# A third pair of places for split weight halves in two mixers, taken from tiles that lose their second buffer

## The chip, the core and the metric

The kernel runs on one core of a Trainium2 chip. Its time is the device time of one execution in microseconds (us); several executions are given by their median. TensorE (PE) multiplies matrices, VectorE (DVE) and ScalarE (ACT) work element by element, GpSimd (POOL) does little here, and SyncE (SP) issues the transfers from HBM.

## The reference, cut to what matters

The model runs 256 tokens of width 1024 through two blocks. The first block (a gated linear attention with pooling, then a mixture of 32 experts) takes the first 850 us and holds nothing of what this change is about. The second block has two layers. Each is a mixer and then a feed-forward part:

```python
p = x_normed @ w_in                    # 1024 -> 3788 columns, split into 16 parts
o_delta = gated_deltanet(q, k, v, z, b, a, ...)    # convolution of 4 taps and silu on q, k, v; then
    # chunks of 64: T = inverse(I + strict(beta k k^T decay)), u0 = T (beta v), wk = T (beta e^G k)
    # a scan over 4 chunks: u = u0 - wk S; o = q_dec S + (q k^T decay) u; S = g S + k_dec^T u
o_sparse = dsa_attention(q, k, v, qi, ki, wi)      # scores of an indexer, top 64, softmax
o_gated  = hgrn2(q, f, i, g, lb, norm_g)           # gated linear attention, chunks of 64
x = x + norm(concat(o_delta, o_sparse, o_gated) @ w_out)
x = x + norm(conv_geglu_ffn(norm(x)))
```

All of it is in float32 and has to be accurate to float32.

## The kernel before

A product in full precision on PE would take four passes, so `dense` and `down` split both operands into a high and a low half of a reduced type (fp32r) and add three products: high x high, high x low, low x high. The activations are split once per layer (`hh`, `hl`). The weights come through a ring of 1 MB tiles `w` of 128 x 2048, one for each group of 256 output columns, and each tile is split in two halves of 128 x 1024 that ACT and DVE make: `hl` hands out a pair (`whi`, `wlo`), `split` has ACT copy the weight to `whi` (line 175, which rounds) and DVE subtract it for `wlo` (line 177). One half feeds 24 matmuls of 256 columns (4 of the 8 groups of 128 input rows, two blocks of 128 outputs or tokens, three products), so a step of 256 columns has 48. The pair comes from the pool `spl`, which holds two of them: a new split waits for the matmuls that read the pair two splits earlier.

A mixer is written as a list of steps, among them the dense ones: k0, k1, q0, q1, v0, v1 (the delta rule's, with a convolution at their end), z0, z1, qi, bq, ci, cq, cg, and steps of work between: gates, inv (the inverse by doubling, matrices of 128 x 128), rest and chunks (the delta rule), sp0, sp1 (the sparse attention), hg (the gated linear attention). `order` gives each step a priority, and a scheduler then sorts the instructions of each engine by priority among those whose operands and buffers are ready. A change of the number of buffers thus changes the order on every engine. Each engine works off its queue in order, and an instruction that waits holds up everything behind it.

Four steps of a mixer matter below. At its start PE runs k0 and k1 while ACT computes the delta rule's gates (`E`, `eG` and others, lines 1596 to 1614). In `ci` the result of a dense step is copied from PSUM by ACT (line 1550). A convolution (`conv`, lines 1453 to 1460) takes a result out of PSUM in ACT and DVE, in part through a tile `raw`. In hg, six levels (2, 4, 8, 16, 32 and 64 tokens) each multiply `hq` by `hk` into two PSUM banks, and DVE copies the results under a mask into `hA` (lines 1906 and 1908), after it made the next level's `hq` and `hk` (lines 1912 to 1921).

The PSUM banks of a mixer are dealt out by user: `dense=(0, 1), delta=(2, 3, 4), hgrn=(5, 6), sparse=(7, 6), out=(0, 1, 6, 7)`. All other tiles of a mixer lie in the pool `mp`, with one buffer for each tag unless said.

Of the kernel before, what the change touches and what calls it, by code (L numbers as in the profile page):

```python
# [9 lines left out]
F32 = mybir.dt.float32  # L10
F32R = mybir.dt.float32r
BF16 = mybir.dt.bfloat16
# [5 lines left out]
P = 128  # L18
# [46 lines left out]
class K:  # L65
# [96 lines left out]
    normed0, first = None, []  # L162

    def diag(self, r, first=None):
        dg = self.sml.tile([P, P], F32, name="dg", tag="dg", bufs=2)
        ins = self.nc.vector.tensor_scalar(dg, self.c("ident"), r, None, op0=OP.mult).ins
        if first in self.hold:
            self.normed0 = ins
        return dg
# [3 lines left out]
    def split(self, hi, lo, src):  # L173

        self.nc.scalar.copy(hi, src)  # L175
        with self.tc.issue_after(self.normed0) if self.normed0 else contextlib.nullcontext():
            self.nc.vector.tensor_sub(lo, src, hi.bitcast(F32))  # L177

    def hl(self, shape):
        hi = self.spl.tile([P, 1024], F32R, name="whi", tag="whi")  # L180
        lo = self.spl.tile([P, 1024], F32R, name="wlo", tag="wlo")
        n = shape[0] * shape[1]
        return [t[:, :n].rearrange("p (j c) -> p j c", j=shape[0]) for t in (hi, lo)]

# [1180 lines left out]

    def ffn(self, l, fp, hh, hl, hu, rb):
        nc, v = self.nc, self.v2[l]
        self.ring(dense=(0, 1, 2, 3), out=(4, 5, 6, 7), pre=(2, 3))
        self.tmp = lambda name: fp.tile([P, D], F32, name=name, tag=name, bufs=2)
        late = lambda: fp.tile([P, 2048], F32, name="late", tag="late", bufs=self.lates[1] - 2)  # L1370
        self.late = lambda: (lambda t: (t[:, :D], t[:, D:]))(late())
        uv = self.i["ffn_w_up_2"][l].rearrange("(p j) c -> p j c", j=KJ)

        other = "AB"[self.side == "A"]
        self.wbig = lambda: self.big("w", other, F32).rearrange("p j t -> p (j t)")
        self.first = ["b"] * 2
        dh, dl = (fp.tile([P, 22, S], F32R, name=n) for n in ("dh", "dl"))
        for s in range(11):
            cv = fp.tile([P, 4, S], F32, name="cv", tag="cv", bufs=2)

            def ev(a, q):
                for b in range(2):
                    n = 22 * q + 2 * s + b
                    self.conv(cv[:, 2 * q + b, :], a[:, b, :], [v["fconv"][:, k, n:n + 1] for k in range(3)])
            for q in range(2):
                pc, e = [(q * D_FF + s * 256, 256)], lambda a, q=q: ev(a, q)
                if s < self.plain:
                    def scaled(a):
                        o = self.tmp("xg")[:, :512].rearrange("p (n t) -> p n t", n=2)
                        nc.vector.tensor_tensor(o, a, rb[:, None, :].to_broadcast([P, 2, S]), op=OP.mult)  # L1390
                        e(o)
                    self.dense32(self.wtile(), uv, pc, hu, scaled)
                else:
                    self.dense(uv, pc, (hh, hl), e)
            self.gelu = nc.scalar.activation(cv[:, :2, :], cv[:, :2, :], AF.Gelu_apprx_tanh).ins
            nc.vector.tensor_tensor(cv[:, 2:, :], cv[:, :2, :], cv[:, 2:, :], op=OP.mult)
            d0, d1 = dh[:, 2 * s:2 * s + 2, :], dl[:, 2 * s:2 * s + 2, :]
            nc.scalar.copy(d0, cv[:, 2:, :])
            nc.vector.tensor_tensor(d1, cv[:, 2:, :], d0.bitcast(F32), op=OP.subtract)
        dv = self.i["ffn_w_down_2"][l].rearrange("(j p) c -> p j c", p=P)  # L1400
        return self.down(dv, range(22), dh, dl, "g_ffn_post_2", l, "g_mix_pre_2", l + 1, self.lates[1])
# [60 lines left out]
    def mixer(self, l, mp, hh, hl, hu, rb):  # L1462
        nc, v = self.nc, self.v2[l]
        V = nc.vector
        self.mp = mp
        self.ring(**self.banks)
        self.now = (self.order, self.order2)[l]
        self.tmp = lambda name: T(name, (D,), tag="d4", bufs=N_D4)
# [50 lines left out]
        def load(n, u):  # L1519
            def ev(a):  # L1520
                for b in range(2):
                    c = 2 * u + b
                    self.conv(qkv[n][:, c, :], a[:, b, :],
                              [v["conv"][:, k, 4 * n + c:4 * n + c + 1] for k in range(4)],
                              T("raw", (S,), bufs=2) if b else None)
                x = qkv[n][:, 2 * u:2 * u + 2, :]
                self.silu2(T, x, x)
            self.dense(wv, [(512 * n + 256 * u, 256)], X, ev)
# [99 lines left out]
    def delta_inverse(self, T, kT, gt):  # L1628
# [34 lines left out]
        for m in (1, 2, 4, 8, 16, 32):  # L1663
            for t in range(2):
                ps = self.bk("delta")
                for h in range(4):
                    if m == 1:
                        nc.tensor.transpose(ps[:, h * P:(h + 1) * P], N[:, t, h, :], ident)
                    else:
                        nc.tensor.matmul(ps[:, h * P:(h + 1) * P], N[:, t, h, :], U[:, t, h, :], start=True, stop=True,  # L1670
                                         skip_group_check=True)
                if m == 1:
                    put(Ti[:, t], N[:, t], "lt1", m, 0)
                    put(U[:, t], hv(ps), "lv1", m, 1)
                    continue
                Z = T("Z", (4, P), tag="s2", bufs=4)
                nc.scalar.copy(Z, hv(ps))
                pt, pu = self.bk("delta") if m < 32 else None, self.bk("delta")
                for h in range(4):
                    if m < 32:  # L1680
                        nc.tensor.matmul(pt[:, h * P:(h + 1) * P], Z[:, h, :], Ti[:, t, h, :], start=True, stop=True,  # L1681
                                         skip_group_check=True)
                    nc.tensor.matmul(pu[:, h * P:(h + 1) * P], Ti[:, t, h, :], Z[:, h, :], start=True, stop=True,  # L1683
                                     skip_group_check=True)
                if m < 32:
                    put(Ti[:, t], hv(pt), f"lt{m}", m, 0)
                put(U[:, t], hv(pu), f"lv{m}", m, 1)
# [57 lines left out]
    def delta_chunks(self, T, v, dn, sz, oh, ol):  # L1745
# [6 lines left out]
        for n in range(4):  # L1752
            t, r = n // 2, slice(64 * (n % 2), 64 * (n % 2) + 64)
            u = u0[:, t]
            if St is not None:
                ps = self.bk("delta")
                for h in range(4):
                    nc.tensor.matmul(hv(ps)[r, h, :], wk[:, t, h, r], St[:, h, :], start=True, stop=True,  # L1758
                                     skip_group_check=True)
                V.tensor_tensor(u[r], u[r], hv(ps)[r], op=OP.subtract)  # L1760
            if n < 3:
                ps = self.bk("delta")
                for h in range(4):
                    nc.tensor.matmul(hv(ps)[:, h, :], kd[r, t, h, :], u[r, h, :], start=True, stop=True,
                                     skip_group_check=True)
                S2 = T("S", (4, P), tag="s2", bufs=4)
                if St is None:
                    nc.scalar.copy(S2, hv(ps))
                else:
                    for h in range(4):  # L1770
                        V.scalar_tensor_tensor(S2[:, h, :], St[:, h, :], gl[:, n, h:h + 1], hv(ps)[:, h, :],
                                               op0=OP.mult, op1=OP.add)
            Ss.append(St)
            if n < 3:
                St = S2
            if n % 2:

                po = hv(self.bk("delta"))
                for h in range(4):
                    self.mm(po[:, h, :], qk[:, t, h, :], u[:, h, :], True, False)  # L1780
                    for m in (n - 1, n):
                        if Ss[m] is not None:
                            q = slice(64 * (m % 2), 64 * (m % 2) + 64)
                            self.mm(po[q, h, :], qd[:, h, m * 64:(m + 1) * 64], Ss[m][:, h, :], False, True)
                V.tensor_tensor(o_[:, t], po, rq[:, t, :, None].to_broadcast([P, 4, P]), op=OP.mult)
                self.delta_out(t, T, v, o_, sz, oh, ol)

    def delta_out(self, t, T, v, o_, sz, oh, ol):
        nc, V = self.nc, self.nc.vector
        ss = T("doss", (4,), bufs=2)  # L1790
        for h in range(4):
            scr = T("dscr", (P,), BF16, bufs=2)
            nc.scalar.activation(scr, o_[:, t, h, :], AF.Square, accum_out=ss[:, h:h + 1])
        V.tensor_scalar(ss, ss, P * EPS, None, op0=OP.add)
        y = self.rsq(ss, 0.5 * P ** 0.5)
# [12 lines left out]
    def sparse(self, t, T, bq, kk2, vN, qi, ki2, wi, oh, ol):  # L1808
# [4 lines left out]
        ts = slice(t * P, (t + 1) * P)  # L1813

        def heads(q, k2, func, scale):
            out = T("rl", (4, nk), tag=f"rl{t}")
            ov = out.rearrange("p (n b) k -> p b n k", b=2)
            pss = [self.bk("sparse") for _ in range(2)]
            for pr in range(2):
# [4 lines left out]
                nc.scalar.activation(ov[:, b], pss[b].rearrange("p (n k) -> p n k", n=2)[:, :, :nk], func, scale=scale)  # L1824
            return out
        rl = heads(qi, ki2, AF.Relu, 1.0)
        sc = T("ssc", (nk,), tag=f"ssc{t}")
        V.tensor_scalar(sc, rl[:, 0, :], wi[:, t, 0:1], None, op0=OP.mult)
        for h in range(1, 4):
            V.scalar_tensor_tensor(sc, rl[:, h, :], wi[:, t, h:h + 1], sc, op0=OP.mult, op1=OP.add)  # L1830
# [170 lines left out]
```

## Time and profile before

| | us |
|---|---|
| median of three runs | 1676.02 (1675.28 to 1682.35) |
| the profiled execution | 1677.66 |
| its span on the core | 1675.9 |
| PE busy | 1607.2 (96%) |
| DVE busy | 919.9 (55%) |
| ACT busy | 639.8 (38%) |
| mixer 0 | 873 to about 1069 |
| mixer 1 | 1284 to about 1470 |

The chain that ended last lies on PE for 67% of the span and on line 186, the products of split halves, for 58%. Times below are from the start of the span. A row of a timeline gives start and duration, the instruction with its output and inputs, and in square brackets how long the engine stood idle before it and on what. Matmuls overlap in the pipeline, so their spacing and not their duration counts.

### The profile page before, as it was taken

The numbers are of one execution on the slowest core, as the hardware profiler recorded it, in microseconds if no ns is written. First come the engines' busy times: TensorE is split into PE (matmuls) and PEld (weight loads), VectorE is DVE, ScalarE is ACT, GpSimd is POOL, SyncE is SP. The second block draws the span as 40 slices with busy tenths as digits, with TensorE's granted clock in tenths as the row PEclk, the third lists the DMA queues.
The fourth block names the chain that finished last, engine by engine and source line by source line (L and its number), as shares of the span: only waits on it lengthen the run. The fifth ranks groups of instructions, "written<-read, shape, count | busy, mean of one in ns | idle before, by whom it ended". The sixth has DMA issues, their size and how long they took to land.

```text
span 1675.9 us, 25546 instructions
## 1 busy us (share of the span) xinstructions
PE 1607.2 (96%) x10391; PEld 1211.3 (72%) x10391; DVE 919.9 (55%) x1873; ACT 639.8 (38%) x1102; POOL 21.8 (1%) x54
## 2 busy tenths in 40 slices
PE   7999999998999999999998999999999999999997
PEld 4778788984443344344377898899988989799986
DVE  2665445562212212121166597888847769788865
ACT  3543233441111111011145353555545545355543
POOL 1000000100000000000000000000000000000000
PEclk9999999998999999999999999999999999999999
DMA  8634544797999999999952141545762323425553
GB/s 312 203 119 126 194 158 156 223 394 282 420 421 421 420 420 420 421 421 420 400 176 67 35 151 59 193 152 177 224 213 63 103 73 102 176 97 191 178 188 139
DMA packets 162201, 381.72 MB, mean 228 GB/s; under 512 B 14180, under 2 KB 123308, under 8 KB 135200
## 3 DMA queue, kind: packets, MB, share of 16 engines
q1 hardware_dynamic: 160640, 378.45, 61.4%
q8 instruction: 83, 1.36, 0.3%
q0 software_dynamic: 1008, 1.33, 0.3%
q10 hardware_dynamic: 432, 0.27, 0.1%
q14 instruction: 38, 0.31, 0.1%
HBM read 378.98 MB, written 1.05 MB: 227 GB/s over the span
## 4 chain that ended last, share of the span: by engine, by line
PE 67%; DVE 5%; ACT 3%; issue 1%; DVEq 0%; ACTq 0%
PE bk L186 58%; PE bk L1326 3%; DVE wlo L177 1%; PE bk L1670 1%; PE bk L1683 1%; ACT whi L175 1%; PE bk L1078 1%; PE bk L1681 1%; ACT pscr L151 0%; PE bk L1624 0%; PE bk L1758 0%; DVE ssc L1835 0%; DVE x L1266 0%; PE bk L1283 0%; DVE xg L1273 0%
## 5 line engine op out<-in xcount | busy, mean ns | idle before, releaser
L177 DVE TENSOR_TENSOR wlo<-w,whi 128x1024 fp32r<-128x1024 f32 x236 | 287.8, 1223 | 192.3 <-ACT whi L175 184.6
L175 ACT CAST whi<-w 128x1024 fp32r<-128x1024 f32 x236 | 246.4, 1048 | 298.6 <-PE bk L186 260.0
L186 PE MATMUL bk<-hh,whi 128*128 128x256 f32 x960 | 274.3, 286 | 9.3 <-ACT raw L1456 3.5
L186 PE MATMUL bk<-hh,wlo 128*128 128x256 f32 x960 | 273.9, 286 | 4.7 <-DVE wlo L177 4.7
L186 PE MATMUL bk<-hl,whi 128*128 128x256 f32 x960 | 272.5, 284 | 0.0
L186 PEld LDWEIGHTS bk<-hh,whi 128*128 128x128 f32 x960 | 184.7, 192 | 11.9 <-ACT raw L1456 4.1
L186 PEld LDWEIGHTS bk<-hh,wlo 128*128 128x128 f32 x960 | 184.7, 192 | 7.0 <-DVE wlo L177 5.7
L186 PEld LDWEIGHTS bk<-hl,whi 128*128 128x128 f32 x960 | 184.7, 192 | 0.4
L186 PE MATMUL bk<-w,xg 128*64 128x512 f32 x584 | 156.1, 594 | 2.8 <-ACT xg L1045 2.8
L1068 DVE TENSOR_TENSOR whi<-whi,bk 128x512 f32<-128x512 f32 x16 | 11.0, 688 | 236.6 <-PE bk L186 189.0
L186 PEld LDWEIGHTS bk<-w,xg 128*64 128x64 f32 x584 | 49.3, 137 | 87.7 <-issue 82.7
L186 PE MATMUL bk<-mw,xg 128*64 128x512 f32 x376 | 99.5, 594 | 1.5 <-ACT xg L1045 1.5
L186 PE MATMUL bk<-w,whi 128*64 128x512 f32 x296 | 95.5, 598 | 0.0
L1460 DVE SCALAR_TENSOR_TENSOR cv<-bk,fc,cv 128x255 f32<-128x255 f32 (+1 forms) x160 | 76.7, 479 | 2.8
L186 PEld LDWEIGHTS bk<-mw,xg 128*64 128x64 f32 x376 | 31.7, 137 | 52.5 <-issue 48.6
L186 PE MATMUL bk<-ah,whi 128*128 128x256 f32 x224 | 65.2, 291 | 3.9 <-ACT whi L175 3.9
L186 PE MATMUL bk<-al,whi 128*128 128x256 f32 x224 | 64.3, 287 | 0.0
L186 PE MATMUL bk<-ah,wlo 128*128 128x256 f32 x224 | 64.2, 288 | 0.0
L186 PE MATMUL bk<-whi,ah 128*128 128x256 f32 x224 | 64.1, 288 | 0.0
L186 PE MATMUL bk<-wlo,ah 128*128 128x256 f32 x224 | 64.0, 286 | 0.0
L186 PE MATMUL bk<-whi,al 128*128 128x256 f32 x224 | 63.4, 284 | 0.0
L1326 PE MATMUL bk<-hu,w 128*128 128x128 f32 (+1 forms) x512 | 60.7, 276 | 0.5 <-ACT hu L1287 0.5
(567 smaller groups left out, 3122.8 us busy)
## 6 DMA issues: line engine op xcount, KB each, us to landing
w<-in_moe_w SPq DMA_DIRECT2D x110, 1024.0 KB, 19.8
mw<-in_moe_w SPq DMA_DIRECT2D x66, 1024.0 KB, 19.8
w<-in_w_in SPq DMA_DIRECT2D x50, 1024.0 KB, 5.6
w<-in_ffn_w_up SPq DMA_DIRECT2D x44, 1024.0 KB, 5.4
w<-in_w_mod SPq DMA_DIRECT2D x24, 1024.0 KB, 5.0
w<-in_ffn_w_down SPq DMA_DIRECT2D x22, 1024.0 KB, 4.9
x<-in_moe_w SPq DMA_DIRECT2D x10, 1024.0 KB, 19.8
w<-in_w_out SPq DMA_DIRECT2D x8, 1024.0 KB, 5.8
```

Of the source, the lines that this page charges most:

```text
L175: self.nc.scalar.copy(hi, src)
L177: self.nc.vector.tensor_sub(lo, src, hi.bitcast(F32))
L186: return self.nc.tensor.matmul(out, l, r, start=start, stop=stop, skip_group_check=True)
L1068: V.tensor_tensor(hid, hid, h[1], op=OP.mult)
L1078: nc.tensor.transpose(ps[:, j * P:(j + 1) * P], sh[:, :512].rearrange("s (p j) -> s j p", j=4)[:, j, :], self.c("ident"))
L1326: self.nc.tensor.matmul(a[:m, n * S + t * P:n * S + (t + 1) * P], w[:, k, s0:s0 + m], X[:, k, ts], start=k == 0, stop=k == KJ - 1, skip_gr ...
L1460: eng.scalar_tensor_tensor(out[:, d:], ps[:, :S - d], taps[k], out[:, d:], op0=OP.mult, op1=OP.add)
L1670: nc.tensor.matmul(ps[:, h * P:(h + 1) * P], N[:, t, h, :], U[:, t, h, :], start=True, stop=True, skip_group_check=True)
L1681: nc.tensor.matmul(pt[:, h * P:(h + 1) * P], Z[:, h, :], Ti[:, t, h, :], start=True, stop=True, skip_group_check=True)
L1683: nc.tensor.matmul(pu[:, h * P:(h + 1) * P], Ti[:, t, h, :], Z[:, h, :], start=True, stop=True, skip_group_check=True)
```

## The change

`hl` counts its calls; in a mixer every third pair comes from the pool `mp` instead of `spl`, which makes three pairs in turn. In the feed-forward parts it is as before. The room in memory comes from five kinds of tiles that had two buffers (or a fourth) and have one fewer: the diagonal tile `dg`, the convolution's copy `raw`, `s2` (of which `Z` and `S` are taken), the squares `dscr`, and the tiles `rl` and `ssc` of the two halves of the sparse attention. No instruction is added or removed.

```diff
@@ diag @@
-        dg = self.sml.tile([P, P], F32, name="dg", tag="dg", bufs=2)
+        dg = self.sml.tile([P, P], F32, name="dg", tag="dg", bufs=1)
@@ hl @@
+    third, turn3 = None, 0
+
     def hl(self, shape):
-        hi = self.spl.tile([P, 1024], F32R, name="whi", tag="whi")
-        lo = self.spl.tile([P, 1024], F32R, name="wlo", tag="wlo")
+        self.turn3 += 1
+        pool = self.third if self.third and self.turn3 % 3 == 0 else self.spl
+        hi = pool.tile([P, 1024], F32R, name="whi", tag="whi")
+        lo = pool.tile([P, 1024], F32R, name="wlo", tag="wlo")
@@ ffn @@
+        self.third = None
@@ mixer @@
-        self.mp = mp
+        self.mp = self.third = mp
@@ load (in mixer) @@
-                              T("raw", (S,), bufs=2) if b else None)
+                              T("raw", (S,)) if b else None)
@@ delta_inverse @@
-                Z = T("Z", (4, P), tag="s2", bufs=4)
+                Z = T("Z", (4, P), tag="s2", bufs=3)
@@ delta_chunks @@
-                S2 = T("S", (4, P), tag="s2", bufs=4)
+                S2 = T("S", (4, P), tag="s2", bufs=3)
@@ the norm of the delta rule's output @@
-            scr = T("dscr", (P,), BF16, bufs=2)
+            scr = T("dscr", (P,), BF16)
@@ sparse @@
-            out = T("rl", (4, nk), tag=f"rl{t}")
+            out = T("rl", (4, S), tag="rl")[:, :, :nk]
-        sc = T("ssc", (nk,), tag=f"ssc{t}")
+        sc = T("ssc", (S,), tag="ssc")[:, :nk]
```

On SP, one transfer of `w_out` in each layer moves ahead of one of the feed-forward weights. On ACT, DVE and PE the order of the mixers changes in many places; three of them follow.

ACT at the start of mixer 0, from the split of the normed tokens (`hh`) to the first of the gates (`bt`). The casts `whi<-w` are the high halves of k0, and in the changed kernel of k1 too. Before:

```order
L1295 COPY rb<-bk_6195 128x128
L1300 CAST hh<-whi 128x4x128 x2
L1295 COPY rb<-bk_6219 128x128
L175 CAST whi<-w 128x1024
L1300 CAST hh<-whi 128x4x128 x2
L175 CAST whi<-w 128x1024
L1506 COPY kk_6262<-bk_6314 64x256
L1506 COPY ki_6263<-bk_6314 64x256
L1585 ACTIVATE bt<-baN 128x8
```

and after:

```order
L175 CAST whi<-w 128x1024
L1299 COPY rb<-bk_6195 128x128
L1304 CAST hh<-whi 128x4x128 x2
L1299 COPY rb<-bk_6219 128x128
L175 CAST whi<-w 128x1024
L1304 CAST hh<-whi 128x4x128 x2
L175 CAST whi<-w 128x1024
L1511 COPY kk_6262<-bk_6314 64x256
L1511 COPY ki_6263<-bk_6314 64x256
L1590 ACTIVATE bt<-baN 128x8
```

There are three casts ahead of the gates instead of two; the third is the first half of k1, which before stood behind the gates, two casts in a row.

PE at the end of mixer 0, between two levels of hg (`hq`, `hk`). Before (`vb`, `U`, `kb`, `kd`, `dsq` are the delta rule's):

```order
L186 MATMUL bk_7966<-hq_7959,hk_7960 128x128
L186 MATMUL bk_7967<-hq_7959,hk_7960 128x128
L1624 MATMUL bk_7406<-cst,dsq 128x1 x8
L1733 MATMUL bk_7430<-vb,U 128x128 x3
L1738 MATMUL bk_7436<-U,kb 128x128 x4
L1738 MATMUL bk_7449<-U,kb 128x128
L186 MATMUL bk_7986<-hq_7979,hk_7980 128x128
L186 MATMUL bk_7987<-hq_7979,hk_7980 128x128
```

and after (`bk_7520` is the result of z0):

```order
L190 MATMUL bk_7966<-hq_7959,hk_7960 128x128
L190 MATMUL bk_7967<-hq_7959,hk_7960 128x128
L190 MATMUL bk_7520<-whi,hl 128x256
L190 MATMUL bk_7520<-whi,hh 128x256
L190 MATMUL bk_7520<-wlo,hh 128x256
L190 MATMUL bk_7520<-whi,hl 128x256
L1726 MATMUL bk_7390<-dqkv 128x128
L190 MATMUL bk_7986<-hq_7979,hk_7980 128x128 x2
```

The products of the delta rule have left the place between the levels, and a few matmuls of z0 and one of `dqkv` stand there.

DVE in the same place, from a level's copies into `hA` on. Before:

```order
L1908 COPY_PREDICATED hA_7914<-cst_6253,bk_7926 128x512
L1908 COPY_PREDICATED hA_7915<-cst_6253,bk_7927 128x512
L1912 TENSOR_TENSOR hd<-hB 128x512
L1723 TENSOR_TENSOR qk<-bk_7390,E 128x512
L1906 COPY_PREDICATED hA_7914<-cst_6253,bk_7946 128x64x4
L1906 COPY_PREDICATED hA_7915<-cst_6253,bk_7947 128x64x4
L1724 TENSOR_TENSOR qk<-qk,cst 128x512
L1723 TENSOR_TENSOR qk<-bk_7397,E 128x512
L1920 TENSOR_TENSOR hq_7979<-hk_7980,cq 128x512
```

and after:

```order
L177 TENSOR_TENSOR wlo<-w,whi 128x1024
L1913 COPY_PREDICATED hA_7914<-cst_6253,bk_7926 128x512
L1913 COPY_PREDICATED hA_7915<-cst_6253,bk_7927 128x512
L1917 TENSOR_TENSOR hd<-hB 128x512
L1911 COPY_PREDICATED hA_7914<-cst_6253,bk_7946 128x64x4
L1911 COPY_PREDICATED hA_7915<-cst_6253,bk_7947 128x64x4
L1925 TENSOR_TENSOR hq_7979<-hk_7980,cq 128x512
L1917 TENSOR_TENSOR hd<-hB 128x512
L1926 TENSOR_TENSOR hk_7980<-hk_7980,hk 128x512
```

The low half of cg stands ahead of the first copies, and the delta rule's `qk` has moved behind the levels.

## Rows read from the trace of the kernel before

**Rows 1.** Stretches: PE, PEld, DVE, ACT, POOL busy (count), PE clock, DMA share, GB/s

```profile
873.00:903.00 30.00, 23.64 (x181) 22.63 (x180) 17.13 (x32) 19.37 (x40) 0.00 (x0) 0.94 0.22 70
...
1008.00:1055.00 47.00, 46.19 (x359) 38.28 (x358) 35.15 (x101) 17.51 (x39) 0.00 (x0) 0.96 0.32 113
884.00:892.00 8.00, 6.25 (x37) 6.05 (x38) 7.75 (x11) 4.96 (x10) 0.00 (x0) 0.79 0.00 0
1284.00:1310.00 26.00, 23.82 (x194) 22.76 (x193) 18.91 (x34) 19.77 (x41) 0.00 (x0) 1.00 0.41 124
```

**Rows 2.** PE's waits in mixer 0, 873 to 1055: total us, times, longest

```profile
PE bk L186 <- DVE wlo L177: 3.6, 4, 1.6
PE bk L186 <- ACT whi L175: 2.5, 3, 2.0
PE bk L186 <- ACT raw L1456: 1.9, 2, 1.7
PE bk L186 <- ACT ci L1550: 1.6, 1, 1.6
PE bk L186 <- ACT qi L1543: 1.5, 1, 1.5
PE bk L186 <- DVE hA L1908: 0.4, 1, 0.4
```

**Rows 3.** PE's waits in mixer 1, 1284 to 1458

```profile
PE bk L186 <- ACT raw L1456: 2.1, 3, 1.7
PE bk L186 <- DVE wlo L177: 1.7, 3, 0.8
```

**Rows 4.** Timeline of PE: from k0 to k1 in mixer 0; behind ci in mixer 1

```profile
881.02 0.28 PE L186 MATMUL bk<-hl,whi 128*128 128x256 f32 x1
881.14 0.28 PE L186 MATMUL bk<-hh,wlo 128*128 128x256 f32 x1
883.43 0.39 PE L186 MATMUL bk<-hh,whi 128*128 128x256 f32 x1 [2.02 <-ACT whi L175]
...
885.52 0.39 PE L186 MATMUL bk<-hh,wlo 128*128 128x256 f32 x1 [1.58 <-DVE wlo L177]
...
1367.59 0.39 PE L186 MATMUL bk<-hh,whi 128*128 128x256 f32 x1 [1.62 <-ACT ci L1550]
```

**Rows 5.** Timeline of ACT in mixer 0, the gates and the cast behind; then ci

```profile
875.34 0.18 ACT L1596 ACTIVATE eg<-bk 128x8 f32<-128x8 f32 x1 [2.65 <-DVE G L1594]
...
882.35 1.98 ACT L175 CAST whi<-w 128x1024 fp32r<-128x1024 f32 x2
...
961.77 1.04 ACT L175 CAST whi<-w 128x1024 fp32r<-128x1024 f32 x1 [0.17 <-PE bk L186]
962.72 0.58 ACT L1550 COPY ci<-bk 128x512 f32<-128x512 f32 x1
```

**Rows 6.** Timeline of DVE in mixer 0 beside it

```profile
884.25 1.22 DVE L177 TENSOR_TENSOR wlo<-w,whi 128x1024 fp32r<-128x1024 f32 x1
885.38 1.22 DVE L1876 TENSOR_TENSOR_SCAN hB<-m,cf 128x512 f32<-128x512 f32 x1
886.51 0.46 DVE L1460 SCALAR_TENSOR_TENSOR dqkv<-raw,col,dqkv 128x255 f32<-128x255 f32 x1
```

**Rows 7.** Timelines of DVE and PE at the end of mixer 0, the first levels of hg

```profile
1006.39 1.33 DVE L1908 COPY_PREDICATED hA<-cst,bk 128x512 f32<-128x512 int32 x2
1007.61 0.68 DVE L1912 TENSOR_TENSOR hd<-hB 128x512 f32<-128x512 f32 x1
1008.20 0.68 DVE L1723 TENSOR_TENSOR qk<-bk,E 128x512 f32<-128x512 f32 x1
1008.80 0.75 DVE L1906 COPY_PREDICATED hA<-cst,bk 128x256 f32<-128x256 int32 x2
...
1004.48 1.16 PE L186 MATMUL bk<-hq,hk 64*128 64x128 f32 x16
1005.57 1.16 PE L1721 MATMUL bk<-dqkv 128*128 128x128 f32 x8
```

## The prediction

> **What bounds the kernel now.** I read the busy time of the engines by stretch first, then the waits of TensorE (PE) in each of the two mixers, then the timelines around the largest waits. [rows 1] show the stretches: in the first 30 us of mixer 0 PE is busy 23.64, in its last 47 us 46.19; in mixer 1 the first 26 us hold 23.82. So PE is the bound nearly everywhere, and what a change of the splitting can give is what PE stands idle. [rows 2 to 4] say what ended that idle time: in mixer 0 a low half wlo 3.6 us, a high half whi 2.5, a copy raw 1.9, the eviction of ci 1.6, that of qi 1.5; in mixer 1 raw 2.1, wlo 1.7, ci 1.6. These eight rows sum to 16.5 us. The waits that name a split (3.6 + 2.5 + 1.7) are 7.8 us, under 0.5% of the span; 8.4 us is 0.5%, about what a measurement of this kernel can tell from no change. A second loss of mixer 0 is TensorE's clock: granted at 0.79 of full over 8 us [rows 1], so partly at 1.2 instead of 2.4 GHz, around and after the two places where PE had stood idle 2.02 and 1.58 us [rows 4]; that is 8 x 0.21 = 1.7 us.
>
> **Part 1, the start of a mixer.** Matmuls of 256 columns start 0.12 us apart [rows 4], so a half (24 of them) keeps PE for 2.9 us, while ScalarE (ACT) needs about 1.0 for whi and VectorE (DVE) 1.13 for wlo [rows 5, 6]. With two pairs the first half of k1 can only be split once the first half of k0 is read, and by then ACT is in its row of gate activations, from 875.34 to 882.35 [rows 5]. The cast of it stands behind that row, so PE idles 2.02 us for whi and 1.58 for wlo. In the changed order that cast stands ahead of the gates (first place below the diff). I replay what follows with the durations of the rows. PE ends k0 at 881.3 and goes straight on with 24 matmuls of k1 to 884.2. ACT splits qi's first half at 882.35 and k1's second at 883.3, which is there at 884.3 (PE idle 0.2). DVE's low half for qi stands behind about 2.3 us of convolution and cf work that begins at 882 and ends at 885.4 (idle 0.5); 22 matmuls more bring PE to 888.1. The low half of k1's second half is queued behind a scan, three vector operations and two convolution steps and ends at 889.05 (idle 0.75), that of qi's second half, behind one of bq that no wait holds up, at 892.95 (idle 1.25). Together 2.7 us remain of the 6.36 us idle and the 1.7 us of slow clock in that stretch. The 1.5 us for qi's eviction go too, since no cast that has to wait for PE stands ahead of it any longer. I take a gain of **5.0 us** in mixer 0, between 1.0 (bq's low half does hold the queue, one half of 2.9 us plus a split) and 6.4. In mixer 1 the same stretch has 26 - 23.82 = 2.2 us idle at full clock [rows 1]; leaving about 1.0 by the same queues, **1.2 us** (0 to 2.0).
>
> **Part 2, the eviction of ci.** [rows 5] show a cast at 961.77, released by PE, right ahead of ci's copy at 962.72. In the changed order a cast stands there too, but its room is free one half earlier, so it should have run before ci's last matmul. Then PE waits for one copy of 0.58 and its signal, about 0.7 instead of 1.62: 0.9 in each mixer, **1.8 us** together (0 to 2.2).
>
> **Part 3, the waits for raw.** They come from two or three casts, each released by PE, that stand ahead of a convolution's evictions in ACT's queue. In the changed order there are still two casts ahead, and one exponential row of the attention, so I count a loss of 0.4 per mixer, **0.8 us** (from a gain of 3.0, both waits gone, to a loss of 3.0). That raw, the diagonal tile, the squares dscr and the score tiles have one buffer now makes a writer wait for readers: for raw three convolution steps of about 0.4 us, which can be hidden as DVE reads them ahead of the next cast. I count nothing for these and 0 to 2.0 us for the bound; the cover is the two-half lead of the splits, and once that is gone each would cost PE its 0.4 to 1.2 us.
>
> **Part 4, the end of a mixer.** This is where the order changes most (second and third place below the diff). Before, the levels of the gated linear attention (hq x hk into two banks, copied out under a mask into hA) alternate on PE with the delta rule's products. After, they come in a row, with 19 matmuls of z0, seven products of dqkv and two of the output projection between them, and the delta rule follows. Count both engines from the first pair of hA copies to the last. DVE: one pair of 1.33 and five of about 0.7 (each starts when its copy ends) make 4.8, ten vector operations at 0.6 make 6.0, one wlo 1.13, three small ones about 0.4: 12.3 us [rows 7]. PE: five levels at 1.1 make 5.5, z0 19 x 0.12 = 2.3, dqkv 7/4 x 1.1 = 1.9, two products twice as wide 0.5: 10.2 us. Since each level needs its banks copied out and its operands made, PE loses the difference, about 2.1 us, where it now loses 0.44 on hA [rows 2]. The delta rule's chain behind it has as much dense work to lie under as it needs (48 matmuls of cg and the output projection). I take a loss of **2.0 us per mixer, 4.0 in all**. Low end 0 (DVE's queue has slack from the 1.1 us level ahead of it), high end 6 to 7.5 per mixer (below).
>
> **A rule against the trace.** The Trainium skill, page "Perfetto Trace Analysis", section "Identifying Performance Opportunities", says that a gap that repeats on the engine that should be saturated can mean that there is no room for the next tile. By it alone the 7.8 us of split waits would go and the time be 1668.2. By that rule, the trace agrees for the start of a mixer and not for the rest: raw, ci and qi are evictions behind casts in a queue.
>
> **The sum.** -5.0 - 1.2 - 1.8 + 0.8 + 4.0 = -3.2 us. The profiled execution took 1677.66 us (span 1675.9 and 1.76 around it), the median of the three runs is 1676.02, 1.64 below. 1677.66 - 3.2 = 1674.5 in terms of the profiled one, 1672.8 in those of the median; I say **1673.0**.
>
> **Rivals.**
> *A, the forecast (0.48).* Gains at the start, most of them given back at the end. Its own range is 1667 to 1679.
> *B, the end costs nothing (0.22).* The levels' copies keep pace since DVE reaches them early, and the lead of a half also removes the raw waits. -5.0 - 2.0 - 2.2 - 2.0 = -11.2, so 1664.8; with weaker gains 1668. For it: DVE is busy only 35.15 of 47 us at the end [rows 1]. Against: in the trace those levels are already where hA is waited for.
> *C, slower: the two banks of the levels (0.15).* If the copies of one level hold the whole next level on PE, each of five levels shows its 1.1 us or more, and with the start of the row of copies late by a split (the low half of cg stands ahead of them, and its cast waits for z1's last matmul) a mixer loses 6 to 7.5 us. 12 to 15 less the 7.2 us that parts 1 to 3 gain is +4.8 to +7.8: 1681 to 1684. It decides from a loss of 3.6 us per mixer on. For it: DVE's 12.3 against PE's 10.2. Against: the same levels cost 0.44 now.
> The Trainium skill (same page, section "Optimizing Tensor Performance") wants independent groups of matmuls to rotate through PSUM banks so that one is evacuated under the next; two banks for six levels in a row go against that. The trace has it only as the 0.44 us on hA.
> *D, it doesn't do what it says (0.15).* The third pair is free but ACT and DVE reach its halves no earlier, since their queues (19.37 and 17.13 of 30 us busy at the start) and the gates set the time; PE's idle time moves and stays. 1674 to 1678.
>
> **Numbers.** Faster by over 0.5% (under 1667.6): 0.2 from B and a small part of A, 0.24. Slower by over 0.5% (over 1684.4): a half of C, as its price is no surer than 3 us, and a little of A for what no row shows, 0.11. Within: 0.65. The range that holds 8 in 10 leaves a tenth out on either side: 1664 to 1684.
>
> **What the profile after would show.** Step 1: after 873 the waits of 2.02 and 1.58 are gone, bq's matmuls begin some 5 us earlier against the entry of the mixer, and the clock stays full there. Step 2: PE's wait for ci falls to about 0.7. Step 3: waits on raw between 1 and 2 us remain. Step 4: in the mixer's last 50 us, new waits on hA of 0.3 to 0.7 us each, some 2 us per mixer. I am wrong if the waits on hA sum to over 4 us per mixer (C), or if they are as before and those on raw are gone (B), or if wlo of k1 or qi is still waited for 3 us or more (D).

## The result and the profile after

The changed kernel is slower: a median of 1693.17 us (1690.22 to 1697.08, seven runs) against 1676.89 (1675.28 to 1683.02, seven runs), a ratio of 1.0085 with a 95% interval from 1.0071 to 1.0100. The prediction was 1673.0 with a range up to 1684, so it was wrong in sign and in range. The profiled execution took 1690.28 us, 12.6 more than that of before.

| profiled execution, us | before | after |
|---|---|---|
| execution, span | 1677.66, 1675.9 | 1690.28, 1688.5 |
| PE busy | 1607.2 | 1617.1 |
| DVE busy, ACT busy | 919.9, 639.8 | 922.1, 641.0 |
| mean granted clock | 0.989 | 0.983 |
| mixer 0, from the copy of ki to the first `rb` behind it | 207.7 | 213.2 |
| mixer 1, from the copy of ki to the second `rb` behind it | 201.3 | 210.7 |

The head of the page of after:

```profile
span 1688.5 us, 25538 instructions
PE 1617.1 (96%) x10391; PEld 1218.7 (72%) x10391; DVE 922.1 (55%) x1873; ACT 641.0 (38%) x1102; POOL 21.8 (1%) x54
```

As many matmuls and vector operations as before, and up to mixer 0 the two traces agree (its ki is copied at 871.4 and 871.5). So the loss lies in the order of the two mixers. The stretches below are the whole mixers, first of before, then of after. Columns are as in [rows 1].

```profile
871.50:1079.20 207.70, 193.73 (x1467) 174.14 (x1468) 151.88 (x370) 97.81 (x196) 0.00 (x0) 0.98 0.30 97
1281.50:1482.80 201.30, 191.40 (x1484) 172.41 (x1485) 153.39 (x375) 98.71 (x197) 0.00 (x0) 1.00 0.33 106
```

```profile
871.40:1084.60 213.20, 198.66 (x1478) 178.55 (x1479) 152.30 (x369) 97.59 (x194) 0.00 (x0) 0.97 0.30 95
1286.40:1497.10 210.70, 196.62 (x1491) 176.04 (x1492) 154.26 (x375) 98.66 (x197) 0.00 (x0) 0.98 0.32 102
```

What to read from these rows is the length less PE's busy time, its idle time: 13.97 to 14.54 in mixer 0, 9.90 to 14.08 in mixer 1, together 4.8 us more. In mixer 0 the start's gain and the later loss cancel in that sum. PE's busy time grows by 4.9 and 5.2 us. The program has no matmul more, but the two stretches hold 11 and 7 more than before (x1467 to x1478, x1484 to x1491), which stood behind the mixers. Most of the growth is clock. These are the stretches of after at which the granted clock fell, all six of the mixers:

```profile
972.00:978.00 6.00, 6.00 (x40) 6.00 (x39) 4.74 (x11) 2.65 (x6) 0.00 (x0) 0.72 0.44 152
988.00:994.00 6.00, 3.79 (x20) 3.79 (x21) 4.93 (x11) 2.17 (x5) 0.00 (x0) 0.72 0.56 175
1022.00:1028.00 6.00, 6.00 (x36) 5.59 (x36) 3.28 (x22) 1.19 (x3) 0.00 (x0) 0.72 0.52 172
1054.00:1060.00 6.00, 4.90 (x17) 3.95 (x17) 5.62 (x19) 3.67 (x9) 0.00 (x0) 0.72 0.86 289
1388.00:1394.00 6.00, 5.48 (x33) 5.48 (x34) 4.58 (x9) 2.29 (x4) 0.00 (x0) 0.72 0.56 175
1432.00:1438.00 6.00, 6.00 (x44) 5.13 (x43) 4.40 (x14) 0.83 (x2) 0.00 (x0) 0.72 0.01 3
```

A mean of 0.72 lies between full speed (2.4 GHz) and half (1.2 GHz), and 6 x 0.28 is 1.7 us lost, six times 10.2. The mixers of before have two such stretches (mixer 0 has one around the waits of [rows 4], and one from 1012 to 1016, each 4 us at 0.57), 3.4 us. So of the 14.9 us that the two mixers grew, 4.8 are idle time of PE, 6.8 clock, and 3.3 other busy time, by one profile of each kernel. 2.3 us come back outside the mixers, 0.5 of it in the feed-forward part between them; the 18 matmuls that moved are part of the 3.3 and of the 2.3.

PE's waits in mixer 0 of after, 873 to 1060 (total, times, longest), beside [rows 2]:

```profile
PE bk L190 <- ACT raw L1461: 5.0, 3, 2.3
PE bk L190 <- DVE sg L1575: 2.6, 1, 2.6
PE bk L190 <- DVE wlo L177: 1.2, 2, 1.0
PE bk L190 <- ACT whi L175: 1.1, 1, 1.1
...
PE bk L190 <- DVE u L1765: 0.8, 1, 0.8
PE bk L190 <- ACT qi L1548: 0.7, 1, 0.7
PE bk L190 <- DVE hA L1911: 0.6, 2, 0.4
PE bk L190 <- DVE hA L1913: 0.4, 1, 0.4
```

and in mixer 1, 1289 to 1470, beside [rows 3]:

```profile
PE bk L190 <- ACT raw L1461: 5.5, 3, 2.8
PE bk L190 <- ACT ci L1555: 1.6, 1, 1.6
PE bk L190 <- ACT qi L1548: 1.3, 1, 1.3
PE bk L190 <- DVE wlo L177: 0.9, 1, 0.9
```

What the change was after has shrunk: wlo 3.6 to 1.2 and whi 2.5 to 1.1 in mixer 0, wlo 1.7 to 0.9 in mixer 1. The waits for the convolution's copy `raw` went from 1.9 to 5.0 and from 2.1 to 5.5, 6.5 us more in all. One of them shows how. Timeline of ACT in mixer 0 of after, then of DVE, then of PE:

```profile
983.85 2.01 ACT L175 CAST whi<-w 128x1024 fp32r<-128x1024 f32 x2 [1.78 <-PE bk L190]
985.75 0.47 ACT L1458 ACTIVATE dqkv<-bk,col 128x256 f32<-128x256 f32 x1
986.12 1.07 ACT L1857 COPY PT<-bk 128x512 f32<-128x512 f32 x2
987.94 0.37 ACT L1865 CAST oh<-bk 128x256 fp32r<-128x256 f32 x1 [0.75 <-PE bk L1862]
989.42 0.47 ACT L1458 ACTIVATE dqkv<-bk,col 128x256 f32<-128x256 f32 x1 [1.11 <-DVE dqkv L1465]
989.79 0.36 ACT L1461 COPY raw<-bk 128x256 f32<-128x256 f32 x1
...
984.93 2.36 DVE L177 TENSOR_TENSOR wlo<-w,whi 128x1024 fp32r<-128x1024 f32 x2 [0.41 <-ACT whi L175]
987.21 0.47 DVE L1465 SCALAR_TENSOR_TENSOR dqkv<-bk,col,dqkv 128x255 f32<-128x255 f32 x1
...
990.21 0.58 PE L190 MATMUL bk<-whi,hh 128*128 128x256 f32 x1 [2.32 <-ACT raw L1461]
```

Two casts stand ahead of the first eviction (`dqkv` at 985.75) on ACT, and the two subtractions for the same weights stand ahead of the convolution's taps on DVE (`dqkv` at 987.21). The second eviction on ACT waits for those taps (1.11 <-DVE dqkv), the copy `raw` stands behind it, and PE, whose next product needs the bank that `raw` reads, idles 2.32 us. Weights that PE doesn't need yet are split ahead of a result that it needs emptied now. Counted from the copy of ki, 20 casts of weights stand ahead of this first eviction; in the kernel before it is 18, and the other two stand behind it (at 986.52 and 990.38).

Not only casts moved ahead. At the longest of these waits, 2.83 us at 1388.52 in mixer 1, the casts are done before PE stops, and four exponential rows of the sparse attention (`rl`) stand behind them and ahead of `raw`. In the kernel before those rows begin at 1381.21, behind the copy `raw` at 1380.60. ACT in mixer 1 of after:

```profile
1383.40 2.00 ACT L175 CAST whi<-w 128x1024 fp32r<-128x1024 f32 x2
1385.42 0.51 ACT L1847 ACTIVATE rl<-rl,mx 128x256 f32<-128x256 f32 x1
...
1388.12 0.35 ACT L1461 COPY raw<-bk 128x256 f32<-128x256 f32 x1
```

### The profile page after: what moved, and what is told of

The parts are those of the page before. It is cut to its first block, busy times and chain, and to the rows that moved or that the text cites. A ratio compares the mean times of both kernels' runs of the same rounds, so it can differ in the third digit from the quotient of the medians.

```text
span 1688.5 us, 25538 instructions
## 1 busy us (share of the span) xinstructions
PE 1617.1 (96%) x10391; PEld 1218.7 (72%) x10391; DVE 922.1 (55%) x1873; ACT 641.0 (38%) x1102; POOL 21.8 (1%) x54
## 3 DMA queue, kind: packets, MB, share of 16 engines
q0 software_dynamic: 1008, 1.33, 0.3%
## 4 chain that ended last, share of the span: by engine, by line
PE 63%; DVE 7%; ACT 4%; issue 1%; DMA 1%; DVEq 0%; ACTq 0%
PE bk L190 55%; PE bk L1330 2%; DVE wlo L177 1%; PE bk L1688 1%; ACT whi L175 1%; PE bk L1675 1%; PE bk L1082 1%; DVE ssc L1840 1%; PE bk L1686 1%; ACT pscr L151 1%; DMA mw<-in_moe_w 1%; DVE m L1839 0%; DVE dqkv L1465 0%; DVE xg L1277 0%; PE bk L1629 0%
## 5 line engine op out<-in xcount | busy, mean ns | idle before, releaser
L190 PEld LDWEIGHTS bk<-mw,xg 128*64 128x64 f32 x376 | 31.7, 137 | 52.5 <-issue 49.0
```

The source lines that it names most:

```text
L190: return self.nc.tensor.matmul(out, l, r, start=start, stop=stop, skip_group_check=True)
```

## The experiments

The theories, with the letters of the expectations (not those of the prediction's rivals): A, the third pair lets splits of later steps into the queues of ACT and DVE ahead of evictions; B, the tiles that lost a buffer make writers wait; C, the new order is one bad draw among many, with no rule in it; D, the loss is made by the order at the mixer's end. Each batch was timed beside runs of the kernel before on the same chip, which had medians of 1676.89 (changed kernel), 1679.78 (e1 to e3), 1681.11 (e4 to e7) and 1680.34 (e8 to e11), so the ratios are to be compared, not the medians. The last two columns split the mean span of the timed runs by an estimate: span x (1 - mean granted clock) is what the clock cost, and the rest is the span less that.

| kernel | median (runs) | ratio, interval | wait on raw, mixer 0, 1 | clock | rest |
|---|---|---|---|---|---|
| before | 1676.89 (7) | 1 | 1.9, 2.1 | 21 to 24 | 1656 to 1657 |
| changed | 1693.17 (7) | 1.0085, 1.0071 to 1.0100 | 5.0, 5.5 | 28.0 | 1663.5 |
| e1 no third pair, only the cuts | 1676.96 (10) | 0.9976, 0.9962 to 0.9990 | 1.9, 2.1 | 21.3 | 1653.8 |
| e2 third pair in k0, k1, qi, bq | 1684.43 (10) | 1.0037, 1.0016 to 1.0059 | 0.9, 2.3 | 22.7 | 1661.0 |
| e3 third pair in all but these | 1694.97 (7) | 1.0076, 1.0053 to 1.0100 | 0, 9.1 | 31.2 | 1661.8 |
| e4 other phase of the third | 1703.29 (3) | 1.0119, 1.0081 to 1.0158 | 6.2, 14.5 | 31.7 | 1667.2 |
| e5 the last phase | 1699.83 (3) | 1.0144, 1.0057 to 1.0230 | 11.5, 0 | | |
| e6 changed, evictions first | 1691.10 (4) | 1.0057, 1.0039 to 1.0075 | 3.2, 3.3 | 26.6 | 1663.0 |
| e7 only the cuts, evictions first | 1687.65 (9) | 1.0042, 1.0028 to 1.0056 | 1.3, 1.1 | 22.7 | 1663.8 |
| e8 third pair in ci, v1, v0, q1, q0, cq | 1691.54 (5) | 1.0064, 1.0042 to 1.0086 | 0, 7.3 | 24.7 | 1664.6 |
| e9 third pair in the other steps | 1681.98 (10) | 1.0017, 1.0001 to 1.0032 | 0.9, 1.7 | 19.7 | 1661.0 |
| e10 third pair in k0, k1 | 1682.31 (10) | 1.0017, 1.0003 to 1.0030 | 0, 2.0 | 23.9 | 1656.9 |
| e11 before, `dscr` with one buffer | 1672.00 (4) | 0.9950, 0.9930 to 0.9969 | 1.9, 2.2 | 18.8 | 1652.2 |

**e1: the cuts alone.**

```diff
-        self.mp = self.third = mp
+        self.mp = mp
```

> The five tiles have one buffer fewer, as in the change, but there is no third pair. Theory A (the third pair lets splits of later steps stand ahead of evictions in the queues, and the end of a mixer is put in another order): the same as before, -1 to +3 us. Theory B (the tiles that lost a buffer, raw above all, make the evictions wait): most of the loss is here, +10 to +16 us, and the waits of PE on raw are 5 us per mixer as in the changed kernel.

A little faster than before (2.8 us by the medians, just outside A's forecast), and the waits on raw are those of before. B falls: without a third pair the five smaller tiles make nothing wait. The order differs from that of before almost only at the mixers' ends, where the wait on `xg` (1.85 us once in each mixer) shrinks to 0.2. The loss comes with the third pair, and beside e1 it is larger than beside before: 1.0085 against 0.9976, some 18 us.

**e2 and e3: the start alone, and all but the start.** In e2:

```diff
+            self.third = mp if k in ("k0", "k1", "qi", "bq") else None
             with self.level(k):
```

and in e3 with `not in`.

> All of the change, but the third pair is used only in the steps k0, k1, qi and bq of a mixer. Theory A: the 5 us that mixer 0 gains up to bq stay, the end is nearly as before: 3 to 6 us faster than before. Theory B: the loss stays, 8 to 15 us slower than before. A third possibility is that the gain of the start is lost in the stretch behind ci, where DVE is busy 28 of 29 us: within 2 us of before.

> All of the change, but the third pair is used only after k0, k1, qi and bq. Theory A: the loss without the gain, 15 to 22 us slower than before. Theory B: as the changed kernel less its gain, 15 to 20 us slower, which tells it apart only together with the run without a third pair.

e3 has the loss of the whole change (15.2 us by the medians, at the near end of both forecasts), with waits on raw of 9.1 us in mixer 1, none in mixer 0, and the second largest clock loss of the table. So the loss sits in the later steps. e2 has what part 1 of the prediction wanted (from the copy of ki to that of bq 32.8 us instead of 38.7 in mixer 0), PE's waits in that mixer fell from 14.4 to 8.7 us, and still it is not faster but slower, by 4.7 us in the medians, between all three forecasts. The waits don't show it, PE's busy time does, for one in small products of the attention that the new order puts elsewhere. Groups of PE in mixer 0 (busy, mean ns), of before and then of e2:

```profile
L186 PE MATMUL bk<-hqs,hke 64*128 64x128 f32 x24 | 1.9, 290 | 0.0
L1857 PE MATMUL bk<-PT,vN 128*64 128x256 f32 x12 | 1.7, 396 | 0.0
...
L190 PE MATMUL bk<-hqs,hke 64*128 64x128 f32 x24 | 3.9, 356 | 0.5 <-DVE hA L1913 0.5
L1864 PE MATMUL bk<-PT,vN 128*64 128x256 f32 x12 | 3.0, 400 | 0.0
```

The same matmuls, 3.3 us more of busy time in a mixer. In the first group part of it is clock: 8 of the 24 run in a slow stretch (1008 to 1019, granted clock 0.53), where one takes up to 0.58 us against a median of 0.27. The second group has nearly the same mean and 1.3 us more, so its matmuls overlap less with their neighbours. That is a row, not a cause; which neighbour does it wasn't isolated.

**e4 and e5: the other two phases.** The third pair is taken at another one of every three splits.

```diff
-        pool = self.third if self.third and self.turn3 % 3 == 0 else self.spl
+        pool = self.third if self.third and self.turn3 % 3 == 1 else self.spl
```

and `== 2` in e5.

> The changed kernel with the third pair taken in the calls one later (remainder 1 instead of 0), so that the same three pairs go around but other halves sit in the mixers' pool, and the scheduler comes to another order. Theory A (with a third pair, splits of steps of high priority stand ahead of the evictions of steps of low priority, whatever half it is): 10 to 16 us slower than before, waits on raw of 4 to 6 us per mixer. Theory C (the changed kernel has drawn a bad order among many, and the third pair as such costs nothing): anywhere from 6 us faster to 20 slower, and well apart from the changed kernel and from the other phase.

> The same with remainder 2. Theory A: 10 to 16 us slower than before. Theory C: well apart (over 5 us) from the changed kernel or from the run with remainder 1.

Both are slower than before, by 22 and 19 us in the medians, which is more than A's 10 to 16; their intervals overlap that of the changed kernel. (The three runs of e5 were 1696.47, 1699.83 and 1717.84, hence its wide interval and no split.) Three orders, three losses with longer waits on raw: that speaks against C for the sign, as far as three draws can. For the size C stands, since raw takes 10.5, 20.7 and 11.5 us, at different convolutions and in e5 in one mixer only, where A had 4 to 6 in each. PE's wait on raw in mixer 1 of e4:

```profile
PE bk L190 <- ACT raw L1461: 14.5, 3, 5.8
```

**e6 and e7: the convolution's evictions ahead of the splits.** Their priority is put ahead of all else, in e6 in the changed kernel, in e7 without the third pair.

```diff
+        kept = self.tc.cur_priority
+        if ahead:
+            self.tc.cur_priority = self.base - 1000000 + kept % 40000
         ...
+        self.tc.cur_priority = kept
```

> The changed kernel, but the instructions of ACT and DVE that take a convolution's result out of PSUM have a priority ahead of all steps, so that no split that is ready at the same time goes before them. Theory A: the waits of PE on raw fall from 10.5 to under 4 us in all, two or three stretches of slow clock behind them go too, and the kernel comes out 5 to 9 us faster than the changed one, 5 to 9 us slower than before. Theory C: another order, no fixed sign against the changed kernel, and raw waits as long.

> The same priority for a convolution's evictions without a third pair (the five cuts stay). Theory A: with two pairs few splits stand ahead of evictions (raw 4.1 us of waits in all), so 0 to 3 us faster than the kernel with the cuts alone. Theory C: no fixed sign, over 4 us apart from it.

In e6 raw falls from 10.5 to 6.5 us, not to under 4, and the ratio from 1.0085 to 1.0057, about 5 us, with intervals that overlap at their ends; it stays well above 1. Part of the wait has moved, as its list for mixer 1 shows:

```profile
PE bk L190 <- DVE wlo L177: 6.2, 3, 5.1
PE bk L190 <- ACT raw L1464: 3.3, 3, 2.3
```

With the evictions in front the low half comes late, 5.1 us once. e7 missed A's expectation: raw halves (4.0 to 2.4), but the splits are waited for more, and it is slower than e1 by 11 us in the ratios, as C had allowed. So evictions ahead of splits are no remedy either, and an order can cost that much with no third pair in it. In that stretch DVE is nearly full already in the kernel before (the rows stand in part 3 below), and what goes first there chooses who waits.

**e8 and e9: the steps with an eviction of that kind, and the others.** e8 has the third pair in ci, v1, v0, q1, q0 and cq; e9 in k0, k1, qi, bq, z0, z1, cg and the output projection.

```diff
+            self.third = mp if k in ('ci', 'v1', 'v0', 'q1', 'q0', 'cq') else None
             with self.level(k):
```

> The changed kernel with the third pair used only in the steps ci, v1, v0, q1, q0 and cq, where the convolutions are. Theory A (the loss is casts and low halves of a later step that stand ahead of a convolution's evictions on ACT and DVE, and the slow clock behind such waits): waits on raw over 4 us in a mixer, 8 to 15 us slower than before. Rival D (the loss comes with the order of the mixer's end, where the levels of hg and the delta rule are taken apart): 3 us or less slower.

> The complement: the third pair only in k0, k1, qi, bq and in z0, z1, cg and the output projection. Theory A: waits on raw as before (about 2 us per mixer), the start's gain kept: 4 us faster to 3 us slower. Rival D: 8 to 15 us slower.

Measured against before, e8 carries most of the loss and e9, which has all the dense steps of the mixer's end, hardly any: A, not D. Both have the five cuts, though, and beside e1 (0.9976) e8 loses 0.9% and e9 0.4%, so the steps outside the convolutions are not free. In mixer 0 PE doesn't wait on raw in e8 at all; the 7.3 us are mixer 1's. e8 also shows a second form. Timeline of ACT in mixer 1, then PE:

```profile
1385.42 1.05 ACT L175 CAST whi<-w 128x1024 fp32r<-128x1024 f32 x1 [3.58 <-DMA w<-in_w_in]
1386.38 0.47 ACT L1458 ACTIVATE dqkv<-bk,col 128x256 f32<-128x256 f32 x1
...
1391.74 0.58 PE L190 MATMUL bk<-hh,whi 128*128 128x256 f32 x1 [5.11 <-ACT raw L1461]
```

A cast that is so far ahead that its weight has not landed holds ACT for 3.58 us, and the evictions with it (two more casts and four exponential rows follow ahead of `raw`). In the mixers of before ACT waits for no transfer of `w_in` ahead of a cast; in the changed kernel it does so three times:

```profile
ACT whi L175 <- DMA w<-in_w_in: 4.6, 3, 2.0
```

Such a wait of ACT need not reach PE: in the mixers of e9 it adds up to 8.2 us, and PE waits on raw for 2.6 us there, less than in before.

The order can also be counted without a clock. Counted from the start of the program, the copy of ci in mixer 0 has 72 casts of this kind ahead of it in ACT's queue in before, e1, e2, e9, e10 and e11, and 73 in the changed kernel and in e3, e4, e5 and e8 (e6 and e7 reorder ACT themselves and are left out). The first group has ratios from 0.995 to 1.0037, the second from 1.0064 to 1.0144. It is a mark of the order and not a cause by itself: mixer 0 of e3 and of e8 has 73 too, and PE has no wait on raw in it.

**e10: k0 and k1 alone.**

```diff
+            self.third = mp if k in ('k0', 'k1') else None
             with self.level(k):
```

> The third pair only in k0 and k1, that is for one half of weights in each mixer. If the start's gain of the trace (2.0 and 1.6 us of waits and 1.7 us of clock in mixer 0) can be had alone: 2 to 5 us faster than before. If every new order of the instructions behind it costs, as in the run with k0, k1, qi and bq: 2 to 8 us slower.

The waits of mixer 0 fall from 14.4 to 7.5 us, the time does not fall. In the profiled execution the gain is still there at the end of mixer 0 (202.4 us from ki to the first `rb`, against 207.7) and gone in mixer 1 (208.6 against 200.4). There PE is busy 198.0 us instead of 190.5, at a granted clock of 0.97 instead of 1.00, with slow stretches from 1305, 1363 and 1476. Over the ten timed runs the rest is that of before and the clock's part at its upper end. What drives either stays open.

**e11: one cut alone, in the kernel before.**

```diff
-            scr = T("dscr", (P,), BF16, bufs=2)
+            scr = T("dscr", (P,), BF16)
```

> The kernel before with one change: the squares dscr have one buffer. The order of the instructions is then nearly that of the kernel with all five cuts and no third pair, which was 0.24% faster than before. If that gain comes from the order at a mixer's end (the norm behind the output projection starts with 0.25 us of idle PE instead of 1.85): 2 to 5 us faster. If it was chance between runs: within 1 us.

Faster than either kernel. PE's products of `xg` behind the mixer, first in before and then in e11:

```profile
1071.43 1.13 PE L1283 MATMUL bk<-cst,xg 128*128 128x128 f32 x8 [1.85 <-DVE xg L1273]
...
1071.86 0.35 PE L1283 MATMUL bk<-cst,xg 128*128 128x128 f32 x1 [0.25 <-DVE xg L1273]
```

That is 1.6 us in each mixer. The rest of its 0.5% isn't explained by these rows: the estimate puts some 4 us to the rest and some 3 to the clock, over four runs against those of before beside them. One buffer for `dscr` moves the end of the mixer, not the convolutions. Two buffers for `raw` beside the third pair weren't run, so it is not shown that its single buffer costs nothing there too; in after, ACT has no idle time right before any of its twelve copies `raw`.

## Why the prediction was wrong

**Part 1, the start: right, but worth nothing at the end.** The bq of mixer 0 is copied at 905.0 instead of 910.2, 5.2 us earlier against a forecast of 5.0. The waits left are 0.66, 0.28, 0.97 and 0.68, 2.6 us, where 2.7 were counted. That the sums agree is in part luck: 0.66 is on a copy `raw`, which wasn't counted there, and 0.68 on qi's eviction, which was to be gone; of the four waits that were counted, for splits, two are left (0.28 and 0.97). The stretches of [rows 1] read in after:

```profile
873.00:903.00 30.00, 27.34 (x221) 26.05 (x220) 21.03 (x39) 21.93 (x44) 0.00 (x0) 1.00 0.34 106
884.00:892.00 8.00, 6.85 (x51) 6.13 (x50) 8.00 (x12) 6.03 (x12) 0.00 (x0) 1.00 0.00 0
1284.00:1310.00 26.00, 24.43 (x198) 22.96 (x197) 19.81 (x41) 20.28 (x44) 0.00 (x0) 1.00 0.40 122
```

The clock is full there (mixer 1 begins 4.9 us later than before, so its window doesn't hold quite the same work). The 1.7 us of clock that the sum took away is a low draw, however: with the same waits of 2.02 and 1.58 us the profile of e1 has 8, 4 and 11 us at 0.57, 0.57 and 0.53 between 885 and 927, about 10 us lost, and that of e11 about 5. A clock loss read from one profile is good to several us only. In mixer 1 the stretch from ki to bq went from 33.9 to 33.1, 0.8 against 1.2. But e2 and e10, which have this gain and little else, are slower than before or about as fast. The first step that failed is to carry a gain of one stretch to the end of the program with the order behind it taken as given.

**Part 2, the eviction of ci: wrong.** It was to fall to 0.7 in both mixers. PE waits 1.13 for the half behind it in mixer 0 and 1.62, as before, in mixer 1. ACT in mixer 0:

```profile
956.41 1.04 ACT L175 CAST whi<-w 128x1024 fp32r<-128x1024 f32 x1 [1.25 <-PE bk L190]
957.36 0.58 ACT L1555 COPY ci<-bk 128x512 f32<-128x512 f32 x1
```

The cast ahead of ci still waits for PE. The step took it that the same cast stands there with its room free one half earlier. With one more place the order lets one more cast in front (73, not 72), and that one waits for its room again.

**Part 3, the waits on raw: the term that was mis-sized, with the wrong sign of the whole behind it.** A loss of 0.8 us was counted for both mixers, 3.0 as its far end. It is 6.5 us in waits (0.66 of it at the start, counted in part 1 above), and the slow clock at three of them (972, 988 and 1388) adds 5.1 in this profile, which the sum did not hold at all: it took away the clock loss at the start and counted none where new waits come. The replay that was done instruction by instruction for the start ended at bq. For the convolutions the prediction counted the casts in front of a copy on ACT ("still two", and one exponential row, where the longest wait has four) and did not follow DVE's queue, where the taps that the next eviction waits for stand behind two subtractions of 1.2 us each. The single buffers, for which nothing to 2.0 us was kept, cost nothing without a third pair (e1). The stretch from the copy of ci to the last copy `raw` of mixer 0, of before and then of after:

```profile
962.70:991.70 29.00, 26.69 (x216) 25.47 (x216) 27.91 (x56) 15.58 (x30) 0.00 (x0) 1.00 0.45 139
...
957.40:989.80 32.40, 28.11 (x216) 26.74 (x216) 29.29 (x56) 16.17 (x32) 0.00 (x0) 0.95 0.35 106
```

The same 216 matmuls and 56 vector operations take 3.4 us longer: 2.0 more idle on PE (2.31 to 4.29) and 5% of 32.4, 1.6, of clock. DVE, not PE, was the fullest engine here already before, with 27.91 of 29.00 us busy: this row stood in the trace of before, and a plan that adds work in front of DVE's taps should have been priced by it.

**Part 4, the end: the size was near, the place was not.** 2.0 us per mixer on hA were expected. In mixer 0 it is 1.0 instead of 0.4, in mixer 1 PE has no wait on hA left. The larger new wait at the end of mixer 0 is that of 2.61 us on `sg`, which stands in DVE's queue behind a subtraction for the output projection:

```profile
1053.15 1.21 DVE L177 TENSOR_TENSOR tlo<-w,thi 128x1024 fp32r<-128x1024 f32 x1
1054.28 0.68 DVE L1575 SCALAR_TENSOR_TENSOR sg<-th,bk 128x512 f32<-128x512 f32 x1
```

From the first copies into hA to the next layer mixer 0 takes 81.4 us instead of 72.8, with two slow stretches (1022 and 1054) in it where before has one (1012). How much of that the end makes itself is open: e9, with the third pair in all of its steps, is at 1.0017.

**The rivals.** C had the sign, with another mechanism: the two banks of the levels cost 1.0 us, not 12 to 15. B and D are out, as the split waits went and others came. What was missing among them is the slower case that came true: the third pair ahead of the evictions. Part 3 had its pieces and gave it 0.4 us per mixer. What the runs settle is that the loss comes with the third pair (e1) and mostly with its use in the steps ci to cq (e8, e9). That work queued ahead of the evictions makes all of it is not shown: with the evictions put first (e6) about a third of it came back.

The Trainium skill, page "Perfetto Trace Analysis", section "Identifying Performance Opportunities", says that a gap that repeats can mean there is no room for the next tile. The trace agrees as far as the gap goes: given the room, the waits for splits fell (wlo 3.6 to 1.2 and whi 2.5 to 1.1 in mixer 0). That the time falls with the gap (1668.2) was a step beyond that, and here the time rose: the measurement decides.

## What to carry to other kernels

Where a scheduler fills in-order queues by what has room, one more buffer for an early operand is also a licence to queue that work ahead of everything that frees a result. Before such a change, list what then stands between each PSUM eviction and the head of its queue on every engine that the eviction depends on, and price it over the whole loop, not only where the wait was. And try the cuts that were to pay for it alone: here one of them was worth more than the change.

## What the runs showed of the hardware

Four of the six slow stretches of the clock in the mixers of after lie right at or behind a wait of PE of 2.04, 2.32, 2.61 or 2.83 us. But the wait of 2.09 us on raw at 1407 in the same trace has none behind it (granted clock 1.00 from 1404 to 1414), nor have those of 1.62 to 1.66 in both traces. Two (1022 and 1432), and 1012 of before, follow no wait above 1 us. So the wait alone doesn't make a rule. Each stretch cost 1.7 us, nearly as much again as the wait. What one kernel's runs differ by is mostly this too: over the 54 runs of before beside the experiments the clock's part, by the estimate above, went from 13 to 30 us and the rest from 1652 to 1660.

The second surprise is that PE's busy time isn't a constant of the instructions. At the same count the profiled executions of e2, e9 and e10 show 1619.1, 1611.2 and 1614.9 us against 1607.2. The clock's part of these spans, by the estimate above, is 21.9, 16.8 and 20.1 against 18.4, so at an equal clock there are an estimated 8.4, 5.6 and 6.0 us more. Counted in windows of 1 us from mixer 0 on, each at its own clock, it is 8.5, 5.2 and 4.5. That goes with the order of the same instructions, and it is enough to swallow most of a gain of 5 to 6 us of waits.
